# A trunk layer on one core: two column blocks of the second MLP projection as seven half-size products in seven of eight slices

## The chip, the cores and the metric

The kernel runs on one core of one Trainium2 chip. The metric is the device time of one execution in microseconds; the time given for a kernel is the median of its runs. Beside it there is one profiled execution per kernel, whose span, from the first instruction to the last, is a little shorter than its device time.

TensorE (PE in the profile, PEld for its weight loads) multiplies, VectorE (DVE) and ScalarE (ACT) work elementwise, GpSimd (POOL) does small things, and SyncE (SP) issues most of the DMAs from one queue, in order. An engine runs its own instructions in order and waits on semaphores for those of others.

## The reference

One layer of a decoder trunk on 256 positions of width 2048, in fp32: three mixing branches (a gated DeltaNet, an HGRN2 recurrence, an attention into 256 memory tokens), and then an MLP. The change lies in the MLP alone:

```python
h2 = rmsnorm(x, g_pre_mlp[l])
m = jnp.square(jax.nn.relu(h2 @ w_mlp_in[l])) @ w_mlp_out[l]
x = x + rmsnorm(m, g_post_mlp[l])
```

`h2` is 256 x 2048, `w_mlp_in` 2048 x 8192, `w_mlp_out` 8192 x 2048. Each weight is used for 256 rows only.

## The kernel before

**A product.** Weights come in groups: KG = 2 tiles of 128 rows by 512 columns, 512 KB, one DMA on SP (`load_w_raw`, line 186, tile `w`). `split_w` (line 197) makes two tiles out of each: ScalarE casts `wh` = fp32r(w), VectorE subtracts `wl` = w - wh. The activations exist in the same two parts (`mh` and `ml` here). A product is hi x hi + hi x lo + lo x hi, three matmuls that accumulate in PSUM. The pool `wp` holds four buffers each of `w`, `wh` and `wl` (WB = 4): a load waits until the tile's former content is split, a cast or split until TensorE has read the pair's former content.

**The MLP.** It goes in NE = 8 slices of 1024 hidden columns. `mlp_in(e)` is the first projection of slice e, in two units of 512 columns: `unit_stacked` runs over 8 weight groups, two at a time, with the weights as the stationary operand and the activations `h2h` moving; `products_joined` gives each pair of groups 16 matmuls of 512 columns (high part) and 16 of 256 (low part), and turns their order from pair to pair. Then the unit is evacuated: ScalarE copies one half of each of four PSUM tiles, VectorE adds the other (four times 128x256, `relu<-mm,relu`), one VectorE operation of 128x1024 makes relu squared, and ScalarE and VectorE split it into `mh` and `ml`.

`mlp_out(e)` is the second projection of slice e: four column blocks c of 512, each a call of `unit` with 4 groups of 2 k-tiles, for each k-tile 2 row halves with 3 matmuls, 48 matmuls a block. VectorE adds each block's result into `yacc` (slice 0: ScalarE copies). Blocks 0 and 1 use a PSUM tile of two banks, blocks 2 and 3 two single banks.

The loop runs `mlp_in(e)` and then `mlp_out(e - 1)`, so that the evacuation of one stands beside the matmuls of the other; `mlp_out(7)` comes behind the loop, with the RMSNorm and the output (`final`).

**What sets the order.** The code's order is a start; the framework's scheduler moves instructions within each engine's list where data and buffers allow it. Small work (generators in the list `bg`) is issued piece by piece between products by `tick`. The DMA queue of SP goes in order: a load that waits for its buffer holds up those behind it. All the instructions that go through the wrapper `Placed` carry its line, L56, in the profile, so operations are told apart by their tiles.

Of the kernel before, what the change touches and what calls it, by code (L numbers as in the profile page):

```python
# [40 lines left out]
def tile_trunk(ctx: ExitStack, tc, a):  # L41
# [31 lines left out]
    wp = ctx.enter_context(tc.tile_pool(name="wp", bufs=4))  # L73
    hp = ctx.enter_context(tc.tile_pool(name="hp", bufs=4))
    gp = ctx.enter_context(tc.tile_pool(name="gp", bufs=25))
    lp = ctx.enter_context(tc.tile_pool(name="lp", bufs=1))
# [4 lines left out]
    pbp = ctx.enter_context(tc.tile_pool(name="pbp", bufs=4, space=bass.MemoryType.PSUM))  # L81

# [24 lines left out]


# [14 lines left out]
    def load_grow(names, c0, q):  # L123
        grow = const(f"grow{c0}", [len(names) * 16, P])
# [84 lines left out]
    def unit(act, nk, src, c0, r0=0, order=None, split=False, post=None, ws=None):  # L209

        if split:
            ps = [bank("mm") for _ in range(2)]
        else:
            both = pmm.tile([P, 1024], F32, tag="mm", name=nm("mm"))
            ps = [both[:, 0:512], both[:, 512:1024]]
        if order is None:
            order = [(g, None) for g in range(nk // KG)]  # L220
        ws = ws or {}
        for i, (g, tt) in enumerate(order):
            k0 = g * KG
            if g not in ws:
                ws[g] = load_w(src, r0 + k0, KG, c0)
            wh, wl = ws[g]
            for j in range(KG):
                kt = k0 + j
                ah, al = act(kt)
                for t in range(NT) if tt is None else (tt,):  # L230
                    o = ps[t]
                    st, sl = ah[:, t * P:(t + 1) * P], al[:, t * P:(t + 1) * P]
                    T.matmul(o, st, wh[:, j, :], start=kt == 0, stop=False)
                    T.matmul(o, st, wl[:, j, :], start=False, stop=False)
                    T.matmul(o, sl, wh[:, j, :], start=False, stop=kt == nk - 1)
            tick()
            if post is not None and i + 1 in post:
                post[i + 1](ps)
        return ps if split else both
# [20 lines left out]
    def unit_stacked(pairs, nk, src, c0, ps):  # L260

        for gg in range(0, nk // KG, 2):
            groups = []
            for g in (gg, gg + 1):
                k0 = g * KG
                groups.append((k0, load_w(src, k0, KG, c0),
                               [flat(pairs[kt // 4][:, kt % 4]) for kt in range(k0, k0 + KG)]))
            for i, _ in enumerate(products_joined(ps, groups, nk, range(4), gg // 2 % 2)):
                tick(0.5)
# [162 lines left out]
    mgt, mlt, caus = const("mgt", [P, P]), const("mlt", [P, P]), const("caus", [P, P])  # L432
    mgtr, onesr = const("mgtr", [P, P], F32R), const("onesr", [P, P], F32R)
    msk2 = const("msk2", [P, 2, P])
    dblk = const("dblk", [P, BL])

    mblk = const("mblk", [P, P])
    rfirst, rsecond = const("rfirst", [P, 1]), const("rsecond", [P, 1])
    mT = {s: const(f"mT{s}", [P, P]) for s in (1, 2, 4, 8, 16, 32, 64)}

    def gen_masks():
# [12 lines left out]
        for s in (1, 2, 4, 8, 16, 32, 64):  # L454
            b = 2 * s
            if b < P:
                cur = cst.tile([P, P], F32, tag=f"blk{b.bit_length() % 2}", name=f"blk{b}")
# [8 lines left out]
            d = cst.tile([P, P], F32, tag="mdiff", name=f"mdiff{s}")  # L466
# [23 lines left out]
    rbm = const("rbm", [P, S])  # L490
# [13 lines left out]
    def gen_start():  # L504
# [11 lines left out]
        crow = const("crow", [96, P])  # L516
        adma(crow, a["conv_a"][0].rearrange("t (c p) -> (t c) p", p=P))
        lrow = const("lrow", [8, P])
# [78 lines left out]
    ccol = const("ccol", [P, 96])  # L597
    lbl1, lba = const("lbl1", [P, 8]), const("lba", [P, 8])
    gna, gnb = const("gna", [P, P]), const("gnb", [P, P])
    alog, dtb = const("alog", [P, 8]), const("dtb", [P, 8])  # L600
# [87 lines left out]
    beta = const("beta", [P, NT, 8])  # L688
    ld = const("ld", [P, NT, 8])
    ldh, ldl = const("ldh", [P, NT, 8], F32R), const("ldl", [P, NT, 8], F32R)  # L690
# [613 lines left out]
    gbc = load_gbc(a["g_post_mix"])  # L1304

# [79 lines left out]
    st2 = const("st2", [P, 8])  # L1385

    def gen_s2():
        for c in range(4):
            for t in range(NT):
                j = g4("junk")  # L1390
                A.activation(j[:, 0:512], xs[c][:, t, :], AF.Square, accum_out=st2[:, t * 4 + c:t * 4 + c + 1])
            yield
# [6 lines left out]

    h2act = act_of(h2T)  # L1400
    yacc = [None] * 4
# [3 lines left out]
    first = [(g, t) for t in range(NT) for g in range(4)] + [(g, None) for g in range(4, 8)]  # L1405

    def gen_turn(r, hi, lo):
# [3 lines left out]
        for hh in range(2):  # L1411
            for q in range(2):
                for t in range(NT):
# [3 lines left out]
            split_psum(pt[:, hh * 512:(hh + 1) * 512].rearrange("p (q s) -> p q s", q=2),  # L1417
                       hi[:, hh * 2:hh * 2 + 2, :], lo[:, hh * 2:hh * 2 + 2, :])
            yield

    def mlp_in(e):
        mt = []
        for u in range(2):
            c0 = e * 1024 + u * 512
            hi, lo = g4("mh", (P, 4, S), F32R), g4("ml", (P, 4, S), F32R)
            r = g4("relu")
            if e == 0 and u == 0:
                ps = unit(h2act, KT, a["w_mlp_in"][0], c0, order=first, ws=ahead)
                A.activation(r, ps, AF.Relu)
                V.scalar_tensor_tensor(out=r, in0=ps, scalar=0.0, in1=r, op0=ALU.max, op1=ALU.mult)  # L1430
                bg.append(gen_turn(r, hi, lo))
            else:
# [7 lines left out]
                unit_stacked(h2B, KT, a["w_mlp_in"][0], c0, ps)  # L1440
                r4 = r.rearrange("p (c s) -> p c s", c=4)
                for c in range(4):
                    A.copy(r4[:, c, :], ps[c][:, S:2 * S])
                    V.tensor_tensor(out=r4[:, c, :], in0=ps[c][:, 0:S], in1=r4[:, c, :], op=ALU.add)
                V.scalar_tensor_tensor(out=r, in0=r, scalar=0.0, in1=r, op0=ALU.max, op1=ALU.mult)
                split_psum(r4, hi, lo)
            mt.append((hi, lo))
        return mt

    def mlp_evac(c, t, p_):  # L1450
        y_ = yacc[c][:, t, :]
        V.tensor_tensor(out=y_, in0=p_, in1=y_, op=ALU.add)
        j = g4("junk")
        A.activation(j[:, 0:512], y_, AF.Square, accum_out=stf[:, t * 4 + c:t * 4 + c + 1])
        return y_

    def final(ps, t):
        y3 = mlp_evac(3, t, ps[t])
        yg = g4("yg")[:, 0:512]
        V.tensor_tensor(out=yg, in0=y3, in1=gb(3), op=ALU.mult)  # L1460
# [4 lines left out]
        for c in range(4):  # L1465
            x_, y_ = xs[c][:, t, :], yacc[c][:, t, :] if c < 3 else yg
# [3 lines left out]
    def mlp_out(e, mt):  # L1470
        for c in range(4):
            args = (act_of(mt), 8, a["w_mlp_out"][0], c * 512, e * 8)
            if e == NE - 1 and c == 3:
# [3 lines left out]
                          post={4: lambda ps: final(ps, 0)})  # L1477
                final(ps, 1)
                continue
            ps = unit(*args, split=c >= 2)  # L1480
            if c < 2:
                ps = [ps[:, t * 512:(t + 1) * 512] for t in range(NT)]
            if e == 0:
                yacc[c] = g4("yacc", (P, NT, 512))
            for t in range(NT):
                if e == 0:
                    A.copy(yacc[c][:, t, :], ps[t])
                elif e < NE - 1:
                    V.tensor_tensor(out=yacc[c][:, t, :], in0=ps[t], in1=yacc[c][:, t, :], op=ALU.add)
                else:  # L1490
                    y_ = mlp_evac(c, t, ps[t])
                    V.tensor_tensor(out=y_, in0=y_, in1=gb(c), op=ALU.mult)

    prev = mlp_in(0)
    bg.append(gen_s2())
    for e in range(1, NE):
        cur = mlp_in(e)
        if e == 4:
            gbc = load_gbc(a["g_post_mlp"])
        mlp_out(e - 1, prev)  # L1500
        prev = cur
    drain()
    mlp_out(NE - 1, prev)
# [14 lines left out]
```

## Time and profile before

| | |
|---|---|
| median of 3 runs | 1793.82 us (1793.5 to 1794.29) |
| span of the profiled execution | 1792.7 us |
| loads of `w_mlp_in` and `w_mlp_out` | 128 of each, 512 KB |
| DMA over the span | 336.60 MB, mean 188 GB/s |
| splits of weights on VectorE, whole kernel | 610, mean 1220 ns |
| casts of weights on ScalarE, whole kernel | 610, mean 1049 ns |

The profiled execution's span lies 1.1 us below the median of the runs. The rows of groups read: line, engine, operation, tile out <- tiles in, shapes, count, then busy time, mean ns, and the engine's idle time just ahead of them with what ended it. Rows of the timeline read: start, length of the group of alike instructions, engine, line, operation, count, and idle time ahead. Other rows stand where they are used.

### The profile page before, as it was taken

What the parts mean: (1) busy time and instruction counts of PE and PEld (TensorE: products, weight loads), DVE (VectorE), ACT (ScalarE), POOL (GpSimd) and SP (SyncE); (2) the same over time, 40 slices, a digit from 0 to 9 for tenths busy, and PEclk for the clock granted to TensorE, in tenths of its full rate; (3) what the DMA queues carried; (4) which work ended last, traced back from release to release, by engine and by line L of the source; (5) the groups of instructions that cost most, each with busy time, mean ns of one, the idle gap of its engine ahead of it and who ended that gap; (6) DMA issues with size and microseconds to landing.
All of it is one profiled execution on the core that took longest, in us unless ns stands there. A gap on an engine that the chain in (4) does not pass through costs nothing.

```text
span 1792.7 us, 23771 instructions
## 1 busy us (share of the span) xinstructions
PE 1780.9 (99%) x9137; PEld 1517.3 (85%) x9137; DVE 1151.3 (64%) x1599; ACT 905.8 (51%) x1156; POOL 58.6 (3%) x100
## 2 busy tenths in 40 slices
PE   9999999999999999999999999999999999999998
PEld 7888888888888888888888888888888888888886
DVE  5765768684858488688655557655656565655556
ACT  6644666454554475565444445544444444444433
POOL 0000000400030000000000000000000000000000
PEclk9999999999999999999999999999999999999999
DMA  7665555864587465555566665666666575656554
GB/s 265 209 192 165 172 157 165 226 211 153 157 221 211 122 201 167 165 171 173 168 188 211 214 221 165 188 198 188 192 194 190 188 219 185 196 187 199 187 194 136
DMA packets 176226, 336.60 MB, mean 188 GB/s; under 512 B 13656, under 2 KB 15472, under 8 KB 175728
## 3 DMA queue, kind: packets, MB, share of 16 engines
q1 hardware_dynamic: 169280, 325.10, 58.3%
q0 software_dynamic: 2304, 5.44, 1.6%
q10 hardware_dynamic: 4528, 4.54, 0.9%
q8 instruction: 71, 1.16, 0.3%
q14 instruction: 43, 0.35, 0.1%
HBM read 332.75 MB, written 2.29 MB: 187 GB/s over the span
## 4 chain that ended last, share of the span: by engine, by line
PE 84%; ACT 0%; DVE 0%; issue 0%; DVEq 0%; POOLq 0%; POOL 0%
PE mm L56 80%; PE pa L56 1%; PE kk L56 0%; PE bo L56 0%; PE o L56 0%; PE pzt L56 0%; PE pw L56 0%; PE tr L56 0%; PE y L56 0%; PE oT L56 0%; PE mgT L56 0%; ACT L56 0%; PE dec L56 0%; DVE x L56 0%; ACT bd L56 0%
## 5 line engine op out<-in xcount | busy, mean ns | idle before, releaser
L56 DVE TENSOR_TENSOR wl<-w,wh 128x1024 fp32r<-128x1024 f32 (+1 forms) x610 | 738.4, 1220 | 518.7 <-ACT wh L56 446.9
L56 ACT CAST wh<-w 128x1024 fp32r<-128x1024 f32 (+1 forms) x610 | 636.1, 1049 | 719.2 <-PE mm L56 631.1
L56 PE MATMUL mm<-wh,hh 128*128 128x512 f32 x1152 | 366.3, 392 | 0.0
L56 PEld LDWEIGHTS mm<-wh,hh 128*128 128x128 f32 x1152 | 216.1, 188 | 44.7 <-ACT wh L56 0.3
L56 PE MATMUL mm<-wl,hh 128*128 128x512 f32 x576 | 224.5, 390 | 0.0
L56 PE MATMUL mm<-h2h,wh 128*128 128x512 f32 x960 | 224.4, 390 | 0.0
L56 PEld LDWEIGHTS mm<-h2h,wh 128*128 128x128 f32 x960 | 178.3, 188 | 35.8
L56 PE MATMUL mm<-wh,mh 128*128 128x512 f32 x512 | 199.2, 389 | 0.0
L56 PE MATMUL mm<-wl,mh 128*128 128x512 f32 x512 | 199.2, 389 | 0.0
L56 PE MATMUL mm<-wh,ml 128*128 128x512 f32 x512 | 199.2, 389 | 0.0
L56 PE MATMUL mm<-hh,wh 128*128 128x512 f32 x768 | 185.0, 392 | 0.8 <-ACT z L56 0.8
L56 PEld LDWEIGHTS mm<-hh,wh 128*128 128x128 f32 x768 | 140.9, 188 | 28.5 <-ACT z L56 1.0
L56 PEld LDWEIGHTS mm<-wl,hh 128*128 128x128 f32 x576 | 108.2, 188 | 21.1
L56 PEld LDWEIGHTS mm<-h2h,wl 128*128 128x128 f32 x960 | 119.1, 192 | 2.3
L56 PE MATMUL mm<-h2h,wl 128*128 128x256 f32 x960 | 120.2, 283 | 0.0
L56 PEld LDWEIGHTS mm<-wh,ml 128*128 128x128 f32 x512 | 96.1, 188 | 20.0
L56 PEld LDWEIGHTS mm<-wh,mh 128*128 128x128 f32 x512 | 96.1, 188 | 20.0
L56 PEld LDWEIGHTS mm<-wl,mh 128*128 128x128 f32 x512 | 96.1, 188 | 19.8
L56 PEld LDWEIGHTS mm<-hh,wl 128*128 128x128 f32 x768 | 98.7, 191 | 3.4
L56 PE MATMUL mm<-hh,wl 128*128 128x256 f32 x768 | 101.6, 283 | 0.0
L56 PE MATMUL mm<-wh,oh 128*128 128x512 f32 x128 | 50.1, 392 | 0.0
L56 PE MATMUL mm<-wl,oh 128*128 128x512 f32 x128 | 50.0, 390 | 0.2 <-DVE wl L56 0.2
(339 smaller groups left out, 1770.9 us busy)
## 6 DMA issues: line engine op xcount, KB each, us to landing
w<-in_w_in SPq DMA_DIRECT2D x240, 512.0 KB, 4.3
w<-in_w_mlp_in SPq DMA_DIRECT2D x128, 512.0 KB, 3.8
w<-in_w_mlp_out SPq DMA_DIRECT2D x128, 512.0 KB, 3.9
w<-in_w_out SPq DMA_DIRECT2D x32, 512.0 KB, 4.3
w<-in_w_kv_mem SPq DMA_DIRECT2D x30, 512.0 KB, 5.0
w<-in_w_br_c SPq DMA_DIRECT2D x16, 512.0 KB, 3.9
w<-in_w_br_a SPq DMA_DIRECT2D x16, 512.0 KB, 4.5
w<-in_w_br_b SPq DMA_DIRECT2D x16, 512.0 KB, 3.6
```

Source lines behind the costliest of these rows:

```text
L56: ins = op(*args, **kwargs)
```

## The change

For slices 0 to 6, the column blocks 0 and 1 of the second projection are computed together, as a 2 x 2 block product: the rows of the activations in two halves of 128, the 8 k-tiles in two halves of 4, and the 1024 columns in two blocks of 512. Instead of eight half-size products there are seven (Strassen, in Winograd's form). Three products take the weights and activations as they are (`bare`: 0, 1, 2); four take sums (`summed`: 6, 4, 5, 3 in program order). Each product has 4 k-tiles, in two halves d = 0, 1 of KG = 2, so 12 matmuls.

- **Sums of weights** are made by VectorE in place in the raw tiles, four for each d: w22 + w12, w12 + w11 and so on (signs are put into the activations' sums). The summed tiles are then split like others.
- **Sums of activations** (`gen_sums`): four VectorE operations on halves of the relu tiles, then two casts `sh` and two subtractions `sl`, issued in the background while block 3 and the bare products of the slice before run.
- **Accumulation**: seven accumulators `acc` in place of the four `yacc` of columns 0 to 1023, filled by ScalarE copies in slice 0 and VectorE sums behind it. Seven VectorE sums (`joined`) put them together ahead of the last slice.
- **Order of a slice's second projection**: summed products of d = 0, block 2 groups 0 and 1, summed of d = 1, block 2 groups 2 and 3, bare of d = 0, block 3 groups 0 and 1, bare of d = 1, block 3 groups 2 and 3.
- **Rings**: from the second unit of slice 0 on, six raw tiles (`raw0` to `raw5`) and six pairs (`oh0`/`ol0` to `oh5`/`ol5`) replace the four of `w`, `wh`, `wl`. The memory comes from the masks and constants of the mixing stage (`mk`, `lp`), which are closed, and from `wp`. In that unit groups 0 and 1 still load into `w`, and groups 2 and 3 reuse the pairs of groups 0 and 1.
- **x**: `gen_s2` writes x to DRAM (`xd`, four DMAs of 512 KB on SP), and the last slice loads it again (`load_xs`).
- `gen_turn` makes two more copies on ScalarE, the gain `g_post_mlp` is loaded at slice 7 instead of 4, the background list is emptied after each `mlp_in`, and the last slice has a function of its own.

The counts in the program: matmuls of the whole kernel 8925 before and 8841 now; weight loads per slice 32 and 38, of which the second projection has 16 and 22.

The core of the diff:

```diff
+    def wide_ring():
+        for g in range(2):
+            w = load_w_raw(a["w_mlp_in"][0], g * KG, KG, 512)
+            ahead[8 + g] = split_w(w, KG, home=operand)
+        weights.close()
+        wy = ctx.enter_context(tc.tile_pool(name="wy", bufs=1, side="right", reuse_waits="tile"))
+        raws.extend(at(wy, f"raw{i}", F32) for i in range(1, 5))
+        raws.append(g4("raw5", (P, KG, 512)))
+        pairs.extend(pair_at(wy, i) for i in range(2, 6))
+
+    def raw(src, k0, c0):
+        w = raws.pop(0)
+        raws.append(w)
+        nc.sync.dma_start(w, src[k0 * P:(k0 + KG) * P, c0:c0 + 512].rearrange("(k p) n -> p k n", p=P))
+        return w
...
+    def gen_sums(rs, ops):
+        yield
+        x1, x2 = rs
+        t0, t1 = slice(0, P), slice(P, S)
+        V.tensor_tensor(out=x1[:, :, t0], in0=x1[:, :, t0], in1=x1[:, :, t1], op=ALU.subtract)
...
+        for x_ in (x1, x2):
+            hi, lo = g4("sh", (P, 4, S), F32R), g4("sl", (P, 4, S), F32R)
+            split_psum(x_, hi, lo)
+            ops.append((hi, lo))
+            yield
...
+    def seven(e, mt, ops):
...
+        def product(i, w, d):
+            wh, wl = split_w(w, KG, home=operand)
+            for j in range(KG):
+                ah, al = [z[:, d * KG + j, :] for z in acts[i]]
+                begin, end = d == 0 and j == 0, d == 1 and j == KG - 1
+                T.matmul(ps[i], ah, wh[:, j, :], start=begin, stop=False)
+                T.matmul(ps[i], ah, wl[:, j, :], start=False, stop=False)
+                T.matmul(ps[i], al, wh[:, j, :], start=False, stop=end)
+            if d == 1:
+                if e == 0:
+                    A.copy(accs[i], ps[i])
+                else:
+                    V.tensor_tensor(out=accs[i], in0=ps[i], in1=accs[i], op=ALU.add)
+            tick(0.5)
+
+        def summed(d):
...
+            w12, w22, w11, w21 = raw(w_mo, k1, 512), raw(w_mo, k2, 512), raw(w_mo, k1, 0), raw(w_mo, k2, 0)
+            add_w(w22, w22, w12)
+            add_w(w12, w12, w11)
+            product(6, w22, d)
+            add_w(w11, w22, w11)
+            product(4, w12, d)
+            add_w(w21, w11, w21)
+            product(5, w11, d)
+            product(3, w21, d)
+
+        def bare(d):
...
+            product(0, raw(w_mo, k1, 0), d)
+            product(1, raw(w_mo, k2, 0), d)
+            product(2, raw(w_mo, k2, 512), d)
...
+    def mlp_out(e, mt, ops, after):
+        summed, bare = seven(e, mt, ops)
+        for c, part in ((2, summed), (3, bare)):
+            if c == 3 and after is not None:
+                bg.append(after)
+            part(0)
+            ps = unit(act_of(mt), 8, w_mo, c * 512, e * 8, split=True, load=load_in, post={2: lambda ps: part(1)})
...
```

**Where instructions move.** VectorE before, at the end of a first projection's second unit: the four additions are the evacuation, the rows `wl` are splits of weights of the second projection, numbers tell buffers apart.

```order
L56 TENSOR_TENSOR wl_2146_12397<-w_2144_12394,wh_2145_12396 128x1024
L56 TENSOR_TENSOR relu_2106_12161<-mm_2107_12162,relu_2106_12161 128x256
L56 TENSOR_TENSOR relu_2106_12161<-mm_2108_12163,relu_2106_12161 128x256
L56 TENSOR_TENSOR relu_2106_12161<-mm_2109_12164,relu_2106_12161 128x256
L56 TENSOR_TENSOR relu_2106_12161<-mm_2110_12165,relu_2106_12161 128x256
L56 TENSOR_TENSOR wl_2149_12415<-w_2147_12412,wh_2148_12414 128x1024
L56 SCALAR_TENSOR_TENSOR relu_2106_12161<-relu_2106_12161 128x1024
L56 TENSOR_TENSOR wl_2153_12436<-w_2151_12433,wh_2152_12435 128x1024
L56 TENSOR_TENSOR ml_2105_12160<-relu_2106_12161,mh_2104_12159 128x1024
```

One split stands ahead of the evacuation, and splits and the relu alternate behind it. VectorE after, the same place, up to the evacuation: `raw2` holds w12, `raw3` w22, `raw4` w11, `raw5` w21; the first two rows split products 5 and 3 of d = 0, the next two are sums for d = 1.

```order
L56 TENSOR_TENSOR ol4_9706<-raw4_9699,oh4_9705 128x1024
L56 TENSOR_TENSOR ol5_9708<-raw5_1690_9700,oh5_9707 128x1024
L56 TENSOR_TENSOR raw3_9698<-raw3_9698,raw2_9697 128x1024
L56 TENSOR_TENSOR raw2_9697<-raw2_9697,raw4_9699 128x1024
L56 TENSOR_TENSOR ol0_9542<-raw0_9545,oh0_9541 128x1024
L56 TENSOR_TENSOR relu_1776_11351<-mm_1777_11352,relu_1776_11351 128x256
```

The second sum reads `raw4`, which is loaded anew between the first row and that one. Behind the evacuation:

```order
L56 TENSOR_TENSOR ol1_9544<-raw1_9696,oh1_9543 128x1024
L56 SCALAR_TENSOR_TENSOR relu_1776_11351<-relu_1776_11351 128x1024
L56 TENSOR_TENSOR ol2_9702<-raw3_9698,oh2_9701 128x1024
L56 TENSOR_TENSOR raw4_9699<-raw3_9698,raw4_9699 128x1024
L56 TENSOR_TENSOR ml_1775_11350<-relu_1776_11351,mh_1774_11349 128x1024
L56 TENSOR_TENSOR ol3_9704<-raw2_9697,oh3_9703 128x1024
L56 TENSOR_TENSOR raw5_1690_9700<-raw4_9699,raw5_1690_9700 128x1024
L56 TENSOR_TENSOR ol4_9706<-raw4_9699,oh4_9705 128x1024
L56 TENSOR_TENSOR ol0_9542<-raw0_9545,oh0_9541 128x1024
L56 TENSOR_TENSOR ol5_9708<-raw5_1690_9700,oh5_9707 128x1024
```

Ten full-width operations now stand between the evacuation and the pair `ol5` of product 3. TensorE after, where that pair is read: d = 1 of the summed products, behind 24 matmuls of d = 0 and 24 of block 2 (`mm_1781` is product 6, `mm_1782` product 5, `mm_1783` product 3, and `sh`, `sl` are the activations' sums).

```order
L56 MATMUL mm_1781_11519<-oh2_9701,sl_1766_11132 128x512
L56 MATMUL mm_1782_11520<-oh4_9705,sh_1767_11160 128x512
L56 MATMUL mm_1782_11520<-ol4_9706,sh_1767_11160 128x512
L56 MATMUL mm_1782_11520<-oh4_9705,sl_1768_11161 128x512
L56 MATMUL mm_1782_11520<-oh4_9705,sh_1767_11160 128x512
L56 MATMUL mm_1782_11520<-ol4_9706,sh_1767_11160 128x512
L56 MATMUL mm_1782_11520<-oh4_9705,sl_1768_11161 128x512
L56 MATMUL mm_1783_11521<-oh5_9707,mh_1749_10725 128x512
L56 MATMUL mm_1783_11521<-ol5_9708,mh_1749_10725 128x512
```

The scheduler has put product 3 ahead of product 4; six matmuls each of products 6 and 5 come first. In six of the seven slices the order is this one.

More of the change, by code (lines that the diff above doesn't have):

```diff
@@ L106, in const, with mask @@
         return cst.tile(list(shape), dt, tag=name, name=name)
+    def mask(name, shape, dt=F32, tag=None):
+        return mk.tile(list(shape), dt, tag=tag or name, name=name)
     ident = const("ident", [P, P])
@@ L207, in load_w, with unit @@
         return split_w(load_w_raw(src, k0, n, c0, width), n, width, home=home)
-    def unit(act, nk, src, c0, r0=0, order=None, split=False, post=None, ws=None):
+    def unit(act, nk, src, c0, r0=0, order=None, split=False, post=None, ws=None, load=None):
         if split:
@@ L258, in flat, with unit_stacked @@
         return b.rearrange("p s n -> p (s n)")
-    def unit_stacked(pairs, nk, src, c0, ps):
+    def unit_stacked(pairs, nk, src, c0, ps, load, ws):
         for gg in range(0, nk // KG, 2):
@@ L265, in unit_stacked @@
                 k0 = g * KG
-                groups.append((k0, load_w(src, k0, KG, c0),
+                groups.append((k0, ws[g] if g in ws else load(src, k0, c0),
                                [flat(pairs[kt // 4][:, kt % 4]) for kt in range(k0, k0 + KG)]))
@@ L1398, in gen_s2, with at, pair_at, operand @@
         yield
+    def at(pool, tag, dt):
+        return pool.tile([P, KG, 512], dt, tag=tag, name=tag, bufs=1)
+    def pair_at(pool, i):
+        return (at(pool, f"oh{i}", F32R), at(pool, f"ol{i}", F32R))
+    pairs = [pair_at(wx, i) for i in range(2)]
+    raws = [at(wx, "raw0", F32)]
+    def wide_ring():
[7 more added lines that the diff above has]
+        pairs.extend(pair_at(wy, i) for i in range(2, 6))
+    def operand(n):
+        if n == "wh":
+            pairs.append(pairs.pop(0))
+        return pairs[-1][n == "wl"]
+    def raw(src, k0, c0):
[3 more added lines that the diff above has]
+        return w
+    def load_in(src, k0, c0):
+        return split_w(raw(src, k0, c0), KG, home=operand)
     h2act = act_of(h2T)
-    yacc = [None] * 4
     stf = const("stf", [P, 8])
@@ L1445, in mlp_in @@
                 V.scalar_tensor_tensor(out=r, in0=r, scalar=0.0, in1=r, op0=ALU.max, op1=ALU.mult)
-                split_psum(r4, hi, lo)
+                split_psum(r, hi, lo)
             mt.append((hi, lo))
-        return mt
-    def mlp_evac(c, t, p_):
[L1451 to L1455, printed above, removed]
+            rs.append(r)
@@ new lines, in joined, with square @@
+    def joined():
+        a1, a2, a3, a4, a5, a6, a7 = accs[0:7]
+        for o, x_, y_, op in ((a2, a1, a2, ALU.add), (a6, a1, a6, ALU.subtract), (a7, a6, a7, ALU.add),
+                              (a6, a5, a6, ALU.subtract), (a3, a6, a3, ALU.add), (a4, a7, a4, ALU.add),
+                              (a5, a5, a7, ALU.subtract)):
+            V.tensor_tensor(out=o, in0=x_, in1=y_, op=op)
+        return [[a2, a4], [a3, a5]]
+    yacc = [None] * 4
+    def square(c, t):
+        j = g4("junk")
+        A.activation(j[:, 0:512], yacc[c][t], AF.Square, accum_out=stf[:, t * 4 + c:t * 4 + c + 1])
```

175 lines of the change are left out of this document (117 added, 58 removed).

## The prediction

> **What bounds the kernel now.** I read the page from the top: the span, the busy shares of the engines, and the row of the granted clock.
>
> ```profile
> span 1792.7 us, 23771 instructions
> PE 1780.9 (99%) x9137; PEld 1517.3 (85%) x9137; DVE 1151.3 (64%) x1599; ACT 905.8 (51%) x1156; POOL 58.6 (3%) x100
> PEclk9999999999999999999999999999999999999999
> PE 84%; ACT 0%; DVE 0%; issue 0%; DVEq 0%; POOLq 0%; POOL 0%
> ```
>
> TensorE is busy 99% of the span, its clock stands at the top digit in all forty slices, and the chain that ended last names it for 84% and no other engine for a whole per cent. An average can hide a stage with another limit, so the second view is that of the waits, for TensorE over the whole run.
>
> ```profile
> PE idle L56 <- POOL ident L111: 1.6, 1, 1.6
> PE mm L56 <- DVE memT L56: 0.8, 1, 0.8
> PE mm L56 <- ACT z L56: 0.8, 1, 0.8
> PE mm L56 <- DVE wl L56: 0.2, 1, 0.2
> ```
>
> That is all of it: 3.4 us of waits, none of them in the MLP's slices. Third view: stretches. The first row below is the start of the kernel, where DMA is at its busiest, the second 88 us of the MLP, the length of one slice (columns: us, then busy us of PE, PEld, DVE, ACT, POOL with the count, granted clock, DMA share, GB/s).
>
> ```profile
> 0.00:45.00 45.00, 42.60 (x200) 35.07 (x201) 26.72 (x51) 30.45 (x61) 4.45 (x17) 1.00 0.80 265
> 1376.00:1464.00 88.00, 88.00 (x450) 75.44 (x449) 50.83 (x52) 37.85 (x43) 0.00 (x0) 1.00 0.65 204
> ```
>
> In the MLP TensorE is busy for all of the 88.00 us, VectorE for 50.83 and ScalarE for 37.85, at clock 1.00. So a matmul that goes takes its whole time out of the span, and VectorE has 37 us a slice to spare, as long as what it gets comes early enough.
>
> **The term that is removed.** The timeline of TensorE gives the pitch of a matmul of 512 columns and the length of a first projection.
>
> ```profile
> 1388.67 0.62 PE L56 MATMUL mm<-h2h,wh 128*128 128x512 f32 x2
> ...
> 1414.53 4.00 PE L56 MATMUL mm<-h2h,wl 128*128 128x256 f32 x32
> 1418.36 7.44 PE L56 MATMUL mm<-h2h,wh 128*128 128x512 f32 x32
> 1425.64 4.00 PE L56 MATMUL mm<-h2h,wl 128*128 128x256 f32 x32
> 1429.47 3.82 PE L56 MATMUL mm<-h2h,wh 128*128 128x512 f32 x16
> 1433.13 0.39 PE L56 MATMUL mm<-wh,mh 128*128 128x512 f32 x1
> ...
> 1439.93 0.39 PE L56 MATMUL mm<-wh,mh 128*128 128x512 f32 x1
> ```
>
> From 1433.13 to 1439.93 there are 30 matmuls of the second projection: 6.80 / 30 = 0.2267 us each (a row's 0.39 is the pipelined time of one). Two column blocks of a slice take 2 x 48 = 96 such matmuls, seven products 7 x 12 = 84. So 12 go per slice, 84 in seven slices: 84 x 0.2267 = **19.0 us**. The first projection of a slice, 1388.67 to 1433.13 = 44.5 us, keeps its matmuls; with 192 x 0.2267 = 43.5 a slice is 88.0 us now, and 44.5 + 180 x 0.2267 = 85.3 after.
>
> **What is added on the engines beside it.** The groups of the stretch from 1100 us to the end give the durations (busy us, mean ns, idle time before).
>
> ```profile
> L56 DVE TENSOR_TENSOR wl<-w,wh 128x1024 fp32r<-128x1024 f32 x246 | 299.2, 1224 | 277.1 <-ACT wh L56 227.2 <-PE mm L56 45.7 <-issue 2.4
> L56 DVE TENSOR_TENSOR yacc<-mm,yacc 128x512 f32<-128x512 f32 x56 | 36.1, 685 | 7.4 <-PE mm L56 7.4
> L56 DVE TENSOR_TENSOR ml<-mT,mh 128x512 fp32r<-128x512 f32 x2 | 1.4, 688 | 0.2 <-ACT mh L56 0.2
> L56 ACT CAST wh<-w 128x1024 fp32r<-128x1024 f32 x246 | 259.0, 1054 | 358.5 <-PE mm L56 335.5 <-issue 22.1 <-ACT junk L56 1.0
> ```
>
> A slice gains 6 splits (22 for the second projection, 14 for products and 8 for columns 2 and 3, where 16 stand now), 8 sums of weights and 2 subtractions for the activation sums, 16 x 1.224 = 19.6 us of VectorE, and 4 half sums and 3 more accumulations, 7 x 0.685 = 4.8. No row shows a sum of two fp32 weight tiles; it has the shape and operand count of the split, so I take the split's 1.22, with the same operation at half size (0.688) as the lower bound and two splits as the upper. VectorE comes to 50.8 + 24.4 = 75.2 of 85.3 us, ScalarE to 37.9 + 8 x 1.054 = 46.3. Neither passes TensorE on the mean; what decides is the place.
>
> **The tightest place.** Call T the instant at which the first projection's second unit hands over to the products (1433.13 in this trace). VectorE and ScalarE around it:
>
> ```profile
> 1426.85 2.36 DVE L56 TENSOR_TENSOR wl<-w,wh 128x1024 fp32r<-128x1024 f32 x2 [2.28 <-PE mm L56]
> 1432.60 1.23 DVE L56 TENSOR_TENSOR wl<-w,wh 128x1024 fp32r<-128x1024 f32 x1 [3.39 <-ACT wh L56]
> 1433.74 1.41 DVE L56 TENSOR_TENSOR relu<-mm,relu 128x256 f32<-128x256 f32 x4
> 1435.07 1.22 DVE L56 TENSOR_TENSOR wl<-w,wh 128x1024 fp32r<-128x1024 f32 x1
> 1436.20 1.22 DVE L56 SCALAR_TENSOR_TENSOR relu<-relu 128x1024 f32<-128x1024 f32 x1
> 1437.34 1.22 DVE L56 TENSOR_TENSOR wl<-w,wh 128x1024 fp32r<-128x1024 f32 x1
> ```
>
> The evacuation of the four banks starts at T+0.61 and lasts until T+1.94; full-width operations then start 1.13 us apart. In the changed order ten such operations follow the evacuation, and the tenth makes ol5, the low part for product 3 of the second half. It starts at T+1.94 + 9 x 1.13 = T+12.11 and is done at T+13.33. TensorE has 24 products' matmuls, 24 of column 2 and 12 more ahead of product 3, and reads ol5 in the second matmul after these: 61 x 0.2267 = T+13.83. The **margin is 0.5 us**. Without the lead of six, that is, without the six sums and five splits that VectorE does before T, there would be none: 12 us of it would fall behind T.
>
> What can shift the evacuation is a load. The tile of w11 (raw4) is refilled for the second half once product 5 of the first half is split. TensorE gives that pair free at T-6.5 (1425.64 + 0.96, a quarter of the narrow run of 32); the first of the two splits at 1426.85 stands at just this release today, done at T-5.05. The load is issued there, and the sum that needs it stands ahead of one split and the evacuation. So the evacuation starts no sooner than T-5.05 + L + 2 x 1.13 = T + L - 2.78, with L the time to landing. Landing times (last column) of one load issued in just that moment today, of all of this array, and of the two slowest of 512 KB, with the row of GB/s of the first 45 us:
>
> ```profile
> w<-in_w_mlp_out SPq DMA_DIRECT2D x1, 512.0 KB, 3.7
> w<-in_w_mlp_out SPq DMA_DIRECT2D x128, 512.0 KB, 3.9
> GB/s 0 56 240 174 213 185 376 398 391 369 382 390 386 382 391 390 375 375 109 87 282 153 264 178 0 124 337 138 240 282 314 334 393 302 301 304 293 144 308 233
> w<-in_w_kv_mem SPq DMA_DIRECT2D x15, 512.0 KB, 6.3
> mem<-in_mem SPq DMA_DIRECT2D x2, 512.0 KB, 7.5
> ```
>
> At 3.7 the evacuation moves to T+0.92, 0.31 late, within the margin: no stall. The bound on the other side is the start of the kernel, where loads run back to back at 370 to 398 GB/s and land after 6.3 or 7.5. After the change a slice loads 38 x 0.524 MB in 85.3 us, 234 GB/s, and its second projection 22 in 40.8 us, 283 GB/s, between the 204 of today's slice and those. So L lies between 3.7 and about 5; nearest to the place are the first two rows, since the loads just before T are issued at the same releases as now. I take 4.2: shift 0.81, stall 0.3 us a slice, 7 x 0.3 = **2.2 us**.
>
> **Other edits.** At the first slice's second unit, groups 2 and 3 reuse the pairs of groups 0 and 1: after a group's narrow half (8 of 32 in 3.83 us, 0.96) TensorE needs a pair that VectorE still splits (1.22, with a 0.69 subtraction between): 0.3 to 1.1 us, taken as **0.8**, bounds 0 and 2. The seven joining sums, 7 x 0.69 = 4.8 us, lie beside the last slice's first column block, 48 x 0.2267 = 10.9 us; their first reader is that block's evacuation, so nothing, and 4.8 us if the cover were gone. Four writes of x to DRAM stand on SP's queue ahead of two loads of that unit, and four reloads behind loads that run six ahead; all 512 KB, 2.1 MB each way, against a queue that now waits for VectorE: nothing, at worst one landing (4 to 7 us) each. The move of the gain's load and the two copies per half on ScalarE fall where it is half idle: nothing. The tail after the last matmul is the same:
>
> ```profile
> 1783.86 0.39 PE L56 MATMUL mm<-wh,ml 128*128 128x512 f32 x1
> ```
>
> From there the span has 8.8 us left, before and after.
>
> **A rule against this change.** The trace starts full-width VectorE operations 1.13 us apart though one lasts 1.22, and four evacuations take 1.33 us from first start to next operation. The Trainium skill, "VectorE: DVE Perf Modes", section "The DRAIN you can't avoid", says that the next operation does not start until the pipe of the one before is empty. Where that held, each would cost its full time; the rows above speak against it for independent neighbours, but a sum followed by what reads it has no row here. I weigh it as a rival.
>
> **The sum.** The profiled execution's 1792.7 is 1.1 below the median of the runs, 1793.8, to which I apply the differences: 1793.8 - 19.0 + 2.2 + 0.8 = **1777.8 us**.
>
> **Rivals.**
> - *VectorE at full durations.* If the ten operations behind T start 1.22 apart, and the four evacuations at 4 x 0.417 = 1.67, ol5 comes 9 x 0.09 + 0.34 = 1.15 us later:
>
> ```profile
> L56 DVE TENSOR_TENSOR relu<-mm,relu 128x256 f32<-128x256 f32 x60 | 21.8, 417 | 0.0
> ```
>
> With L at 4.2 the stall is 0.81 + 1.15 - 0.5 = 1.46 a slice, 10.2 us: 1785.8. For it: the sums in place form a chain (raw3, raw4, raw5). Against: the evacuations, each followed by the next, already overlap. Handovers between ScalarE's cast and VectorE's split, a few tenths each, would give the same figure.
> - *The loads take the gain.* At L = 6.3 the shift is 2.91, the stall 2.41, 16.9 us in seven slices: 1792.5, no change. For it: more loads in flight by six tiles. Against: SP's loads before T keep their spacing, and the single one lands in 3.7.
> - *Slower.* The same place with L at the slowest row, 7.5: shift 4.11, stall 3.61, 25.3 us: 1793.8 - 18.2 + 25.3 = 1800.9. It decides from L = 6.5 (2.6 x 7 = 18.2 eats all), and by over 0.2% from 7.0.
> - *The change does not do what it says*: excluded, since TensorE's order holds 84 matmuls fewer.
>
> **How the numbers follow.** A measurement of this kernel can tell about 0.2%, 3.6 us, from no change: 1790.2 to 1797.4. The forecast, stalls from none to 1.2 us a slice, 1774 to 1784: 0.70. VectorE at full durations or late handovers, 1784 to 1790: 0.14. Loads that take all, within 0.2%: 0.08. Slower: 0.08. The range of 8 in 10 takes the first case whole and most of the second: 1773.5 (all hidden, and half a microsecond of spread) to 1788.
>
> **What would show it.** The profile after should have 84 matmuls fewer in the program, about 40.8 us from a slice's first product to its last matmul, VectorE near 75 of 85 us. Right: waits of TensorE of under a microsecond, about one a slice, on ol5 or oh5 in the second half of the summed products, and one near 0.8 in the first slice. Loads of the second projection near 4 us. Wrong: a wait of 2 us or more a slice on the same tile, with the sum of raw2 and raw4 waiting for a DMA (loads) or with full-width operations 1.22 or more apart (VectorE); waits at column 3, where I see over a microsecond of margin; or a clock below 1.00.

## The result and the profile after

The changed kernel takes 1810.27 us (median of 4 runs, 1809.77 to 1810.92) against 1793.79 for the kernel before on the same chip: 1.0092 times the time, 95% interval 1.0078 to 1.0106. The forecast of 1777.8 and its whole range lay on the other side.

The page of the changed kernel, in the rows that were read first before:

```profile
span 1808.6 us, 23962 instructions
PE 1796.2 (99%) x9053; PEld 1498.4 (83%) x9053; DVE 1303.3 (72%) x1764; ACT 961.0 (53%) x1217; POOL 57.9 (3%) x100
PEclk9999999999999999999999999999999999999999
```

84 matmuls are gone (9137 to 9053), and TensorE is busy 15 us longer, not 19 shorter. The clock is what it was. The waits of TensorE, the place where the forecast looked for a loss:

```profile
PE idle L56 <- POOL ident L118: 1.6, 1, 1.6
PE mm L56 <- DVE memT L56: 0.7, 1, 0.7
PE mm L56 <- ACT z L56: 0.7, 1, 0.7
PE mm L56 <- DVE ol L56: 0.4, 1, 0.4
PE mm L56 <- DVE sum L56: 0.2, 1, 0.2
```

3.6 us in all, against 3.4 before. So the loss is not in TensorE's waits: each matmul takes longer. The first matmul on `h2h`, where the MLP begins, and the last matmul, in the timeline of the changed kernel, and the first one of the kernel before:

```profile
1097.67 0.39 PE L56 MATMUL mm<-wh,h2h 128*128 128x512 f32 x1
...
1799.72 0.40 PE L56 MATMUL mm<-oh,ml 128*128 128x512 f32 x1
```

```profile
1076.93 0.40 PE L56 MATMUL mm<-wh,h2h 128*128 128x512 f32 x1
```

The MLP begins 20.7 us later, though up to there TensorE, VectorE, ScalarE and GpSimd run the same instructions in the same order (only SyncE's queue differs, by two loads of `w_mlp_in` that are issued early). From there to the last matmul it is 702.1 us against 1783.86 - 1076.93 = 706.9: only 4.9 of the 19.0 are left. Groups of matmuls, before and after (busy us, mean ns): the wide ones with `hh`, which belong to the mixing stage that the change does not touch, and the narrow ones of the MLP's first projection, whose low parts are called `wl` before and `ol` after:

```profile
L56 PE MATMUL mm<-wh,hh 128*128 128x512 f32 x1152 | 366.3, 392 | 0.0
...
L56 PE MATMUL mm<-h2h,wl 128*128 128x256 f32 x960 | 120.2, 283 | 0.0
```

```profile
L56 PE MATMUL mm<-wh,hh 128*128 128x512 f32 x1152 | 373.0, 398 | 0.0
...
L56 PE MATMUL mm<-h2h,ol 128*128 128x256 f32 x960 | 119.0, 281 | 0.4 <-DVE ol L56 0.4
```

And a first projection in the timeline of the changed kernel:

```profile
1596.77 3.92 PE L56 MATMUL mm<-h2h,ol 128*128 128x256 f32 x32
1600.53 7.57 PE L56 MATMUL mm<-h2h,oh 128*128 128x512 f32 x32
1607.94 3.95 PE L56 MATMUL mm<-h2h,ol 128*128 128x256 f32 x32
1611.73 7.66 PE L56 MATMUL mm<-h2h,oh 128*128 128x512 f32 x32
1619.23 3.97 PE L56 MATMUL mm<-h2h,ol 128*128 128x256 f32 x32
```

A run of 32 wide matmuls took 7.28 us before (1418.36 to 1425.64) and takes 7.41 and 7.50 here, up to 7 ns more each; a run of 32 narrow ones takes 3.76 and 3.79 instead of 3.83. The narrow ones are shorter, and the granted clock is 0.999 in both kernels, so the clock is not the cause. What differs from the first microsecond on is where tiles lie. In the programs' tables of memory, every large tile of the kernel before starts at 192 modulo 256 bytes of its partition. In the changed one, activations start at 128, `oh0`, `ol0`, `oh1`, `ol1` too, but `wp` and `wy`, which are filled from the right end of SBUF, start at 224.

### The profile page after: what moved, and what is told of

It is laid out like the page before. It is cut to its first block, busy times and chain, and to the rows that moved or that the text cites. A ratio compares the mean times of both kernels' runs of the same rounds, so it can differ in the third digit from the quotient of the medians.

```text
span 1808.6 us, 23962 instructions
## 1 busy us (share of the span) xinstructions
PE 1796.2 (99%) x9053; PEld 1498.4 (83%) x9053; DVE 1303.3 (72%) x1764; ACT 961.0 (53%) x1217; POOL 57.9 (3%) x100
## 4 chain that ended last, share of the span: by engine, by line
PE 82%; DVE 2%; issue 1%; DMA 0%; ACT 0%; DVEq 0%; POOLq 0%; POOL 0%
PE mm L56 78%; PE pa L56 1%; DVE ol L56 1%; PE kk L56 0%; DMA raw<-in_w_mlp_out 0%; PE bo L56 0%; PE o L56 0%; DVE relu L56 0%; PE pw L56 0%; PE pzt L56 0%; PE tr L56 0%; PE y L56 0%; PE mgT L56 0%; PE oT L56 0%; DVE raw L56 0%
## 5 line engine op out<-in xcount | busy, mean ns | idle before, releaser
L56 DVE TENSOR_TENSOR wl<-w,wh 128x1024 fp32r<-128x1024 f32 (+1 forms) x362 | 436.9, 1216 | 255.5 <-ACT wh L56 230.6
L56 ACT CAST wh<-w 128x1024 fp32r<-128x1024 f32 (+1 forms) x362 | 374.4, 1045 | 376.3 <-PE mm L56 327.1
L56 ACT CAST oh<-raw 128x1024 fp32r<-128x1024 f32 x288 | 299.6, 1051 | 285.6 <-PE mm L56 221.1
L56 DVE TENSOR_TENSOR ol<-raw,oh 128x1024 fp32r<-128x1024 f32 x288 | 342.7, 1218 | 104.4 <-ACT oh L56 70.3
L56 PE MATMUL mm<-h2h,oh 128*128 128x512 f32 x960 | 228.9, 394 | 0.0
L56 PEld LDWEIGHTS mm<-h2h,oh 128*128 128x128 f32 x960 | 178.5, 188 | 39.8
L56 PE MATMUL mm<-ol,mh 128*128 128x512 f32 x372 | 146.8, 395 | 0.2
L56 PE MATMUL mm<-oh,mh 128*128 128x512 f32 x372 | 146.2, 393 | 0.0
L56 PE MATMUL mm<-oh,ml 128*128 128x512 f32 x372 | 146.1, 395 | 0.0
L56 PE MATMUL mm<-h2h,ol 128*128 128x256 f32 x960 | 119.0, 281 | 0.4 <-DVE ol L56 0.4
```

The lines of the kernel that those rows point to most:

```text
L56: ins = op(*args, **kwargs)
```

## The experiments

Each kernel ran beside runs of the kernel before on the same chip, whose medians were 1793.9 to 1794.2 us.

| run | median us | ratio to before | 95% interval |
|---|---|---|---|
| e1_after_aligned | 1792.69 | 0.9991 | 0.9982 to 1.0000 |
| e2_before_w32 | 1825.93 | 1.0178 | 1.0164 to 1.0192 |
| e4_before_act32 | 1826.14 | 1.0179 | 1.0163 to 1.0195 |
| e5_before_right | 1828.71 | 1.0192 | 1.0178 to 1.0206 |
| e6_after_congruent | 1782.67 | 0.9934 | 0.9921 to 0.9948 |
| e7_before_all32 | 1794.42 | 1.0002 | 0.9993 to 1.0011 |
| e8_before_act128 | 1825.26 | 1.0174 | 1.0160 to 1.0188 |
| e9_before_act256 | 1794.00 | 1.0000 | 0.9991 to 1.0009 |
| e10_before_raw32 | 1793.89 | 0.9998 | 0.9989 to 1.0007 |
| e12_before_wl32 | 1814.79 | 1.0117 | 1.0103 to 1.0131 |
| e11_later | 1783.28 | 0.9945 | 0.9931 to 0.9958 |
| e13_pool_sums | 1811.28 | 1.0097 | 1.0081 to 1.0114 |

### Is it the address?

The changed kernel with an empty tile of 32 bytes at the right end:

```diff
+    pad = ctx.enter_context(tc.tile_pool(name="pad", bufs=1, side="right"))
+    pad.tile([P, 8], F32, tag="pad", name="pad")
     weights = ctx.enter_context(ExitStack())
```

> The changed kernel, with 32 bytes more per partition at the right end of SBUF, so that the weight tiles there (raw1 to raw4, oh2/ol2 to oh5/ol5, and w, wh, wl before them) start at multiples of 64 bytes instead of 32 bytes off; nothing else changes. Theory A (start address): a matmul of 512 columns costs about 6.4 ns more when its moving tile or the next one's stationary tile starts 32 bytes off a multiple of 64; 5350 such matmuls in the changed kernel make 34 us, less about 3 us that the narrow ones gain. Then this runs in 1776 to 1783 us, with wide matmuls 0.227 us apart throughout, and waits of TensorE on ol or oh of up to 1 us a slice may come back. Theory B (place: the upper end of SBUF is slower to read) and theory C (more traffic of DMA and VectorE beside TensorE slows its reads): it stays at 1808 to 1813 us, with wide matmuls 0.2335 us apart.

The kernel before, with empty tiles of 32 bytes on both sides of the pool of weights:

```diff
+    pada = ctx.enter_context(tc.tile_pool(name="pada", bufs=1))
+    pada.tile([P, 8], F32, tag="pada", name="pada")
     wp = ctx.enter_context(tc.tile_pool(name="wp", bufs=4))
+    padb = ctx.enter_context(tc.tile_pool(name="padb", bufs=1))
+    padb.tile([P, 8], F32, tag="padb", name="padb")
```

> The kernel before, with the pool of weight tiles moved up by 32 bytes and everything else at a multiple of 64 as it was; the order of every engine is as it was. Theory A: all 6295 wide matmuls have a weight tile as moving or stationary operand, 6295 x 6.4 ns = 40 us, less 4 us of narrow ones: 1824 to 1836 us. Theories B and C: nothing moves, 1792 to 1796 us.

The same two tiles around the pool `hp`. Behind it, `gp` with all other activations moves by 64, which the expectation left out.

> The kernel before, with the pool of the activations hh and h2h moved up by 32 bytes, and the weights where they were. Theory A: about 3550 wide matmuls have hh or h2h as an operand, 3550 x 6.4 ns = 23 us: 1808 to 1822 us. A variant of A in which only tiles that are written while TensorE runs (the weights) matter, and theories B and C: 1792 to 1796 us.

The kernel before with its weights at the right end:

```diff
-    wp = ctx.enter_context(tc.tile_pool(name="wp", bufs=4))
+    wp = ctx.enter_context(tc.tile_pool(name="wp", bufs=4, side="right"))
```

> The kernel before, with the pool of weight tiles at the right end of SBUF, where the change puts it, 32 bytes off a multiple of 64; the order of every engine is as it was. Theories A and B: 1824 to 1836 us, as A expects for the tiles moved by 32 bytes at the left. Theory C: 1792 to 1796 us.

Weights that start 32 bytes off the activations cost the kernel before 32 us at the left of SBUF and 35 us at the right (1825.9, 1828.7). So the place at the right end is worth 2.8 us at most, and the added traffic is not needed for the loss: theories B and C fall. 32 bytes take 17.6 us from the changed kernel. But theory A had 1776 to 1783 there and missed: all starts were multiples of 64, and the mean of the wide matmuls still stood at 395. It missed in e4 as well (1826.1 above its 1822): products of weights that had not moved with `mh`, which had moved by 64, were slow too. Common to all the slow runs is that weights and activations start at different places modulo 256 bytes, 32, 64 or 96 bytes apart.

### Each start, or the difference?

The changed kernel with 96 bytes at the right end (`[P, 24]` in place of `[P, 8]`):

> The changed kernel with 96 bytes more at the right end of SBUF: the weight tiles there start at 384 modulo 512, as the activations and the pairs oh0/ol0 and oh1/ol1 do. Theory D (difference): what matters is the difference between the start of the moving tile and the start of the stationary tile that is loaded beside it, modulo some power of two of 512 or less; where it is zero a wide matmul takes 0.227 us, otherwise 0.229 to 0.236. Then all tiles agree here: wide matmuls 0.227 us apart throughout, and 1774 to 1784 us, the forecast of the record without a loss of pitch. Theory A (each start by itself, modulo 64): as with 32 bytes, where the starts were multiples of 64 too, 1790 to 1795 us.

The kernel before with 32 bytes ahead of `wp` only, so that all large tiles move together:

> The kernel before, with every large tile moved up by 32 bytes together, weights and activations alike. Theory A: every start is now 32 bytes off a multiple of 64, 1824 to 1836 us. Theory D: the differences are what they were, 1792 to 1796 us.

The kernel before with 128, and with 256 bytes ahead of `hp` (`[P, 32]`, `[P, 64]`):

> The kernel before, with the pools of the activations and of all tiles behind them moved up by 128 bytes against the weights. Theory D with a period of 128 bytes or less: 1792 to 1796 us. With a longer period: 1815 to 1832 us. Theory A: 1792 to 1796 us.

> As the run with 128 bytes, with 256. Theory D with a period of 256 bytes or less: 1792 to 1796 us. With a period of 512: 1815 to 1832 us. Theory A: 1792 to 1796 us.

All tiles together by 32 bytes: nothing (1794.42). Activations by 128 bytes: 31 us. By 256: nothing (1794.00). The same group of matmuls with 128 bytes, and with 256:

```profile
L56 PE MATMUL mm<-wh,hh 128*128 128x512 f32 x1152 | 372.1, 397 | 0.0
```

```profile
L56 PE MATMUL mm<-wh,hh 128*128 128x512 f32 x1152 | 366.3, 392 | 0.0
```

So it is the difference that counts, modulo 256 bytes, as theory D had it, and the start by itself, theory A, does not. With all tiles congruent the changed kernel takes 1782.67 us, 27.6 less than as it was written, and is 0.66% faster than the kernel before (0.52 to 0.79%).

### Whose tiles?

The raw tiles `w` in a pool of their own, moved by 32 bytes against all others:

```diff
-        w = wp.tile([P, KG, 512], F32, tag="w", name=nm("w"), bufs=WB)
+        w = wr.tile([P, KG, 512], F32, tag="w", name=nm("w"), bufs=WB)
```

> The kernel before, with only the raw weight tiles w moved by 32 bytes against all others; TensorE does not read them, DMA, ScalarE and VectorE do. Theory D (the two operands of TensorE): 1792 to 1796 us. Theory E (the difference that matters is between what TensorE reads and what the other engines and DMA touch beside it): up to 1826 us, as in the runs where the weights were moved.

The low parts `wl` in such a pool:

```diff
-        wl = home("wl") if home else wp.tile([P, KG, 512], F32R, tag="wl", name=nm("wl"))
+        wl = home("wl") if home else wr.tile([P, KG, 512], F32R, tag="wl", name=nm("wl"))
```

> The kernel before, with only the low parts wl moved by 32 bytes against all other tiles. Theory D: only the 1504 wide matmuls with wl as moving tile lose 6.4 ns each, 9.6 us, and the 1856 narrow ones that load wl gain about 2 ns each, 3.7 us: 1797 to 1803 us; the groups of matmuls with wl moving show 397 to 399 ns and those with wh moving 391 to 393 as before. Theory E: all wide matmuls lose, 1815 to 1830 us.

Moving the raw tiles, which TensorE does not read, costs nothing (1793.89). So it does not matter where the loads write and where ScalarE and VectorE read beside TensorE. Moving `wl` alone cost 20.8 us, where theory D, which looks at the two tiles of each matmul by itself, had 3 to 9. The groups of the kernel before, and of that run:

```profile
L56 PE MATMUL mm<-wl,hh 128*128 128x512 f32 x576 | 224.5, 390 | 0.0
...
L56 PE MATMUL mm<-wh,mh 128*128 128x512 f32 x512 | 199.2, 389 | 0.0
...
L56 PE MATMUL mm<-hh,wh 128*128 128x512 f32 x768 | 185.0, 392 | 0.8 <-ACT z L56 0.8
```

```profile
L56 PE MATMUL mm<-wh,hh 128*128 128x512 f32 x1152 | 370.7, 396 | 0.0
L56 PE MATMUL mm<-wl,hh 128*128 128x512 f32 x576 | 228.5, 397 | 0.0
...
L56 PE MATMUL mm<-wh,mh 128*128 128x512 f32 x512 | 201.6, 394 | 0.0
...
L56 PE MATMUL mm<-hh,wh 128*128 128x512 f32 x768 | 185.6, 392 | 1.1 <-ACT z L56 0.7 <-DVE sum L56 0.4
```

The wide matmuls with `wh` moving, whose own two tiles agree, are slowed where a matmul with `wl` moving stands next to them (392 before, 396 here), and runs of `hh` over `wh` are not (392 in both). So what must agree are the tiles that TensorE reads in neighbouring matmuls, and not only the two of one. Which two of these reads it takes, no run separates.

### What was left of the forecast

In e6_after_congruent the forecast's other steps can be read by themselves. Its waits of TensorE, and the tight place behind the first projection of slice 6: TensorE, VectorE, and the load that was issued at 1597.3 (last column: us to landing).

```profile
PE mm L56 <- DVE ol L56: 3.3, 6, 0.6
```

```profile
1602.33 0.39 PE L56 MATMUL mm<-oh,sh 128*128 128x512 f32 x1
...
1616.20 0.40 PE L56 MATMUL mm<-oh,mh 128*128 128x512 f32 x1
1617.21 0.50 PE L56 MATMUL mm<-ol,mh 128*128 128x512 f32 x1 [0.61 <-DVE ol L56]
```

```profile
1596.06 2.36 DVE L56 TENSOR_TENSOR ol<-raw,oh 128x1024 fp32r<-128x1024 f32 x2 [1.16 <-PE mm L56]
1598.71 1.23 DVE L56 TENSOR_TENSOR raw<-raw,raw 128x1024 f32<-128x1024 f32 x1 [0.29 <-DMA raw<-in_w_mlp_out]
1602.12 1.23 DVE L56 TENSOR_TENSOR raw<-raw,raw 128x1024 f32<-128x1024 f32 x1 [2.18 <-DMA raw<-in_w_mlp_out]
1603.26 1.22 DVE L56 TENSOR_TENSOR ol<-raw,oh 128x1024 fp32r<-128x1024 f32 x1
1604.40 1.41 DVE L56 TENSOR_TENSOR relu<-mm,relu 128x256 f32<-128x256 f32 x4
1605.72 1.21 DVE L56 TENSOR_TENSOR ol<-raw,oh 128x1024 fp32r<-128x1024 f32 x1
...
1613.67 3.48 DVE L56 TENSOR_TENSOR ol<-raw,oh 128x1024 fp32r<-128x1024 f32 x3
```

```profile
raw<-in_w_mlp_out SPq DMA_DIRECT2D x1, 512.0 KB, 4.7
```

T is 1602.33 here. The split of product 5 ends at T-5.05, the load lands 4.7 later, the sum of raw2 and raw4 has waited for it 2.18 us and starts at T-0.2, and the evacuation starts at T+2.07, 1.5 late instead of the 0.8 expected. `ol5`, the last of the three splits from 1613.67, is done at 1617.15, and TensorE, which would have read it at T+13.83 = 1616.16, reads it at 1617.21. From start to start the two matmuls are 1.01 us apart there, 0.78 more than the pitch. The forecast's own chain, with 4.7 in the place of 4.2, gives 4.7 - 2.78 - 0.61 - 0.5 = 0.81. Product 3 waits like this in five of the seven slices; the sixth of the six waits, 0.4 us, is the one that the forecast had put into the second unit of the first slice.

Two attempts on this stall. First, the summed products of d = 1 one group later, on top of the 96 bytes:

```diff
-            ps = unit(act_of(mt), 8, w_mo, c * 512, e * 8, split=True, load=load_in, post={2: lambda ps: part(1)})
+            ps = unit(act_of(mt), 8, w_mo, c * 512, e * 8, split=True, load=load_in, post={3 if c == 2 else 2: lambda ps: part(1)})
```

> The changed kernel with all tiles congruent (96 bytes at the right end), and in addition the summed products of d = 1 behind three groups of column block 2 instead of two. Theory L (the late load of w11 for d = 1 and the chain of VectorE behind it cost about 0.7 us a slice at product 3): 12 matmuls more stand ahead of that product, 2.7 us, for one more split, 1.1 us, so the stalls go, 1775 to 1780 us against the 1782.7 with two groups. Rival (VectorE is short over the whole second projection): the stall comes back at column block 3 or at the end of the summed products, 1781 to 1786 us.

1783.28 against 1782.67, no gain: the rival. The wait on `ol` shrank to 0.8 us and another came, for banks that VectorE empties late into the accumulators (TensorE's waits in that run):

```profile
PE mm L56 <- DVE acc L56: 2.6, 5, 1.0
...
PE mm L56 <- DVE ol L56: 0.8, 2, 0.4
```

Second, the four sums of d = 1 on GpSimd (`add_w` with `G` in place of `V` where d is 1), on top of the 96 bytes:

> The changed kernel with all tiles congruent (96 bytes at the right end), and in addition the four sums of weights of d = 1 on GpSimd instead of VectorE. Theory L (at product 3 the late load of w11 holds up the evacuation, because a sum that waits for it stands ahead of it on VectorE): GpSimd waits in its place, VectorE has four operations of 1.13 us less up to product 3, and the stalls of about 0.7 us a slice go: 1776 to 1780 us against 1782.7. That holds if GpSimd's sum takes less than about 3 us; its select of 128x128 takes 0.28 us, which makes 2.2 us for 128x1024 as an estimate. Rival (GpSimd is slower than that, or holds up VectorE beside it): 1783 to 1810 us, with waits of TensorE on ol of 2 us and more.

1811.28: no gain either, and 1.3 us above even the rival's range. GpSimd's group, and two of VectorE's in the MLP of that run:

```profile
L1523 POOL TENSOR_TENSOR raw<-raw,raw 128x1024 f32<-128x1024 f32 x28 | 81.0, 2892 | 557.8 <-DMA raw<-in_w_mlp_out 556.5
```

```profile
L56 DVE TENSOR_TENSOR ol<-raw,oh 128x1024 fp32r<-128x1024 f32 x288 | 365.1, 1295 | 132.8 <-ACT oh L56 100.8 <-PE mm L56 26.2 <-issue 4.6
...
L56 DVE SCALAR_TENSOR_TENSOR relu<-relu 128x1024 f32<-128x1024 f32 x15 | 33.6, 2240 | 0.0
```

A sum takes GpSimd 2.9 us, within the 3 us that were allowed, but VectorE's operations beside it take longer: the relu of 128x1024 2.24 us on the mean, where it took 1.22. The mean mixes two kinds: the 8 of 15 that no sum on GpSimd overlaps take 1.22 us, the 7 that overlap one 3.41; of the splits, 17 overlap and take 2.52, the other 271 take 1.22. The additions of the evacuation, which read one tile from PSUM, take 0.41 us beside a sum and 0.42 without. The Trainium skill, "GPSIMD Engine Reference", section "Specifications", lists the SBUF interfaces of GpSimd as shared with VectorE where VectorE's instruction has two SBUF inputs; the relu has such inputs, and the row agrees.

VectorE is not the whole of it. In four stretches of that run, 20 us together, TensorE's granted clock is 0.50, and its matmuls are 0.427 us apart; the first of them (columns as in the prediction's table of stretches):

```profile
1276.30:1279.60 3.30, 3.30 (x10) 2.54 (x9) 2.32 (x4) 2.09 (x2) 0.00 (x0) 0.50 0.97 341
```

TensorE is busy for 17.3 us of the four, so about half of that, 8.7 us, is an estimate of what the clock adds to the 28.6 us between this run and e6_after_congruent. TensorE's waits are most of the rest: 11.6 us on `acc` and 10.1 us on `ol`, the longest 2.1 us. Each of the four stretches comes with a stall near 2 us, but stalls as long at 1364 and 1636 us are followed by none, so what lowers the clock is not shown.

## Why the prediction was wrong

**The step that failed** is the first: the first projection "keeps its matmuls", and 84 fewer at 0.2267 us make the saving. The pitch was taken as a property of the matmul, and all that the change does not touch, the mixing stage included, stands in the sum at nothing. The pitch depends on where the tiles lie as well. The change puts the pool of weights at the other end of SBUF, 96 bytes off the activations modulo 256, and a wide matmul then takes up to 7 ns more. The order of instructions, on which the prediction worked, does not show addresses. The price is 27.6 of the 32.5 us between forecast and result, by e6_after_congruent, most of it ahead of the code that the change is about (20.7 us, of which e6 has nothing: its MLP begins at 1076.90).

```profile
1076.90 0.39 PE L56 MATMUL mm<-wh,h2h 128*128 128x512 f32 x1
```

**The saving of 19.0 us** held, with congruent tiles. In e6_after_congruent the means of the wide matmuls are those of before (392 for `mm<-wh,hh`), and the MLP, from that row to the last matmul at 1773.23, is 696.3 us, 10.6 less than before: 19.0, less 8.4 that other things took. Delays of more than 0.06 us behind the pitch, from start to start of TensorE's instructions, add up to 9.0 us there and 1.4 before, so 7.6 of the 8.4 are stalls and late handovers.

```profile
1773.23 0.39 PE L56 MATMUL mm<-oh,ml 128*128 128x512 f32 x1
```

**The tight place** was the right one, and its chain came out to 0.13 us: issue at T-5.05, evacuation at T + L - 2.65 (forecast T + L - 2.78), ten operations 1.13 apart, `ol5` done 11.4 us after the evacuation (1605.72 to 1617.15; forecast T+1.94 to T+13.33). Mis-sized was L: 4.2 was taken, and 4.7 was measured in the place. The same stands for all loads of the second projection in the changed kernel:

```profile
raw<-in_w_mlp_out SPq DMA_DIRECT2D x170, 512.0 KB, 4.7
```

The 3.7 of the row before was of a ring of four and 32 loads a slice; here it is a ring of six and 38, and which of the two lengthens the landing was not separated. By the start times, product 3 lost 4.8 us in five slices, where 2.2 was set, and the first slice's second unit about 0.7, where 0.8 was set. The rest of the 8.4 had no term in the sum: 0.7 us at one handover that waits for the relu tile, and many small delays. With the tiles congruent the kernel lands at 1782.67, 4.9 above the forecast.

**The rivals.** The ten full-width operations behind the evacuation start 1.13 us apart here too, and a sum and the split behind it as well (1602.12, 1603.26), so the rule that each waits for the pipe of the one before does not set their pace. The Trainium skill, "VectorE: DVE Perf Modes", section "The DRAIN you can't avoid", which the prediction cites for that rule, adds that a next operation that is not held starts earlier, and these rows agree. The chain of sums gives one exception. Where the second of two neighbouring sums overwrites what the first reads, the program makes it wait for the first, and the two start 1.25 us apart (2.47 us for both, 1.21 for one):

```profile
1588.86 2.47 DVE L56 TENSOR_TENSOR raw<-raw,raw 128x1024 f32<-128x1024 f32 x2
```

No such pair stands among the ten, and nowhere in the MLP is a sum followed at once by what reads it, so for that case the rival stays untested. The loads did not take the gain at 4.7. The rival of a slower outcome had the sign right, by luck: its time was 1800.9, its landing of 7.5 was 4.7, and in the changed kernel TensorE's one wait on `ol`, 0.4 us, is in the first slice's second unit and none is at product 3. The slower matmuls seem to cover those stalls, as longer slices leave VectorE more time; no run tests that by itself. None of the signs of being wrong that the prediction named was what happened.

**What stays open.** Why tiles that differ modulo 256 bytes slow TensorE's reads, and why the narrow matmuls gain 1 to 2 ns, was not tried. Of the differences, 32, 64, 96 and 128 were seen to cost and 256 not.

## What to carry to other kernels

A change of pools is a change of addresses: list the start of every tile that TensorE reads, modulo 256 bytes, before and after, and pad until they agree; here 96 bytes are worth 27.6 us of 1810. Compare the mean of a group of matmuls that the change does not touch, in a stage that it does not touch, before looking for waits: 392 against 398 ns told in one row that the loss lay neither in the new code nor in a wait. A load that is issued on a deadline is to be costed with the loads that the change itself puts beside it, not with today's landing.

## What the runs showed of the hardware that was not expected

- Wide fp32r matmuls (512 columns) of neighbouring instructions run 0.227 us apart where the tiles that they read start at the same place modulo 256 bytes, and up to 0.234 in the runs of 32 shown where not: 1794.00 us with activations 256 bytes off, 1825.26 with 128. It makes no difference where that place is (all by 32 bytes: 1794.42), nor where the raw tiles lie that only other engines read (1793.89). With 64 bytes the changed kernel lost about 10 us (1792.69 against 1782.67), with 96 bytes 27.6.
- One of the tiles is enough: `wl` alone off by 32 bytes cost 20.8 us (1814.79 against 1794.01), and slowed the matmuls beside those that read it.
- GpSimd's sum of two 128x1024 fp32 tiles took 2.9 us. VectorE's operations with two SBUF inputs that overlapped one took 3.41 us (relu) and 2.52 us (splits) instead of 1.22; its additions with one input in PSUM were not stretched.
- In the same run (e13_pool_sums) TensorE's granted clock fell to 0.50 in four stretches of 3.4 to 6.8 us, though no wait of TensorE was longer than 2.1 us.
